# Sums of squares added on VectorE, and the opening of a decoder kernel ordered by hand

## The chip, the cores and the metric

One core of one Trainium2 chip runs the program. The metric is the device time of one launch in microseconds; several runs give a median. The profile beside it is one execution, recorded engine by engine: TensorE (PE, with its weight loads PEld), VectorE (DVE), ScalarE (ACT), GpSimd (POOL) and the queues that issue transfers (SPq for SyncE's).

## What is computed

Two macaron layers over 256 tokens of width 1024. Each layer is: half-step SwiGLU FFN, token mixer, half-step SwiGLU FFN; the first mixer is a Mamba-2 scan, the second a sliding-window attention on shared keys and values. Every sub-layer starts with an RMS norm, and that is what the change touches:

```python
def rmsnorm(x, g):
    xf = x.astype(jnp.float32)
    y = xf * lax.rsqrt(jnp.mean(xf * xf, axis=-1, keepdims=True) + EPS)
    return (y * g.astype(jnp.float32)).astype(x.dtype)

def swiglu_half_step(h, g, w1, w3, w2):
    u = rmsnorm(h, g)
    return h + FFN_HALF * ((jax.nn.silu(u @ w1) * (u @ w3)) @ w2)
```

with D_MODEL 1024 and D_FF 2816. All arrays are float32.

## The kernel before

**Layout.** The residual stream hT is kept transposed: eight k-steps of 128 features by 256 tokens. Products are made from split operands: each float32 array is split into a high part (float32r, a rounded copy) and a low part (the rest), and one product is three matmuls, high by high, high by low, low by high (`mm3`, `wmm3`, L130 and L136).

**Weights.** They come in units of 2048 columns (1 MB). A `Unit` (L142) takes a raw buffer (three of them), issues its transfer on SyncE's queue, and is split in four parts of 512 columns: ScalarE casts wh (L164), VectorE subtracts to wl (L165). There are eight buffers each of wh and wl, of 1024 columns. A unit can be held (`hold=True`): then its parts are called by hand.

**A norm.** After a sub-layer, `Norm.step` (L259) is called for four pairs b of k-steps: VectorE adds the pair into hT, `split` (L242) makes vh on ScalarE and vl on VectorE from hT times the gain, and `square` (L249) squares the pair on ScalarE into sq, and adds it to the running sum on GpSimd (L255), folding the pair's second half onto the first at the end (L257, called the half addition below). `stats` makes the mean over features with matmuls (`pc`, `token_mean`), adds eps on VectorE (`me`) and raises to the power -1/2 on GpSimd (`rms_rstd`, L208). `scale` spreads the result over the partitions with matmuls (`pb`, `spread`) and copies it to SBUF (rsb). Chunks 0 and 1 of an FFN start on vh and vl, before the scale is known, and are scaled at the gate; later chunks use the normalized uTh and uTl.

**An FFN.** `run_ffn` (L294) runs over eleven chunks of 256 inner features and two halves f of each. `up(c, f)` makes w1 and w3 products in one PSUM tile pm (48 matmuls); `gate` applies silu and the product and splits the result (ghl); `flush` makes the down products into four acc banks. For chunk 0, f = 0 goes k-step by k-step over both weights w, the others weight by weight. `later(n, fn)` puts stats and scale n matmuls further on in TensorE's order: 60 and 84 in most FFNs, 114 and 134 in the first.

**The opening.** x is loaded in two halves into xin, one of the three raw buffers. TensorE transposes it (`turn_x`, four pairs, px), vh and vl are made straight from px, chained with the splits of chunk 0's two held units; pairs 2 and 3 are turned at k-steps 3 and 5 of the first `up`, and at k-step 7 `keep_x` copies px to hT on VectorE and squares hT.

**What sets the order.** A scheduler orders each engine's instructions by program order as priority and by when their data is expected; `issue_after` (and `behind`, `after_mm`) adds an order on one engine by hand. Each engine then works its list strictly in order.

Of the kernel before, what the change touches and what calls it, by code (L numbers as in the profile page):

```python
# [40 lines left out]
def yoco_kernel(ctx: ExitStack, tc: tile.TileContext, a: dict, out: bass.AP):  # L41
# [16 lines left out]
    xin = rawp.tile([P, NT, D], F32, tag="raw", name="xin")  # L58
# [138 lines left out]

    def gain_cols(g):
        n = g.shape[0]
        pg = ps_mm.tile([P, n], F32, tag="mm", name=nm("pg"))  # L200
        nc.tensor.transpose(pg, g, ident[:n, :n])
        gc = const.tile([P, n], F32, name=nm("gcol"))
        nc.scalar.copy(gc, pg)
        gcols.append(gc)

    def rms_rstd(ms_ap, w, name):
        r = sb.tile([P, w], F32, tag=f"rstd{w}", name=nm(name), bufs=2)
        nc.gpsimd.tensor_tensor(out=r, in0=ms_ap, in1=mhalf[:, :w], op=ALU.pow)  # L208
        return r
# [21 lines left out]
    class Norm:  # L231
        def __init__(self, gi, k0):
            self.gi, self.k0 = gi, k0
# [33 lines left out]
        def stats(self):  # L267
            pc = token_mean(self.sq, 0)
            self.me = sb.tile([P, NT], F32, tag="me", name=nm("me"), bufs=2)
            nc.vector.tensor_scalar_add(self.me, pc, EPS)  # L270
            self.rs = rms_rstd(self.me, NT, "rs")

        def keep_eps(self):
            self.eps = const.tile([P, NT], F32, name=nm("eps"))
            nc.vector.tensor_scalar_mul(self.eps, self.me, EPS)
            self.rsk = const.tile([P, NT], F32, name=nm("rsk"))
            nc.vector.tensor_copy(self.rsk, self.rs)
# [16 lines left out]
    def run_ffn(layer, j, cur, nxt, hook=None, ups=None, at=(60, 84), pre=None):  # L294
# [34 lines left out]

        def up(c, f):  # L330
            u = units(c)
            xh, xl = (cur.vh, cur.vl) if c < 2 else (uTh, uTl)
            pool, tag = (ps_acc, "acc") if c == 0 and f == 0 else (ps_mm, "mm")
            pm = pool.tile([P, 512], F32, tag=tag, name=nm("pm"))

            def one(k, w, first, stop):
                wh, wl = u[k // 4].get((k % 4) * 512 + w * 256 + f * P, P)
                wmm3(pm[:, w * 256:(w + 1) * 256], wh, wl, xh[:, k, :], xl[:, k, :], first, stop)

            if c == 0 and f == 0:  # L340
                for k in range(KT):
                    if pre and k in pre:
                        pre[k]()
                    for w in range(2):
                        one(k, w, k == 0 and w == 0, k == KT - 1 and w == 1)
            else:
                for w in range(2):
                    for k in range(KT):
                        one(k, w, k == 0, k == KT - 1)
# [35 lines left out]
        def start_gates(pm):  # L385
            if hook is not None:
                cur.keep_eps()
            pend.append((0, 0, gate(0, g00)))
            pend.append((0, 1, gate(0, pm)))
            cur.normalize()  # L390

        slow = at[1] > 96
        for c in range(NCHUNK):
            for f in range(2):
                if c == 0 and f == 0:
                    later(*stats)
                    later(*scale)
                    with tc.issue_after(pe[-1]) if pe else nullcontext():
                        g00 = up(c, f)
                    continue  # L400
                pm = up(c, f)
                if c == 0 and not slow:
                    start_gates(pm)
                if c == 0:
                    g01 = pm
                    continue
                if slow and c == 1 and f == 0:
                    start_gates(g01)
# [35 lines left out]
    def mamba(mp, cur, nxt):  # L444
# [299 lines left out]
        def y_stats(g):  # L744
            pc = token_mean(st[g][1], 1)
            me = sb.tile([P, NT], F32, tag="me", name=nm("me"), bufs=2)
            nc.vector.tensor_scalar_add(me, pc, EPS)
            st[g] = (st[g][0], rms_rstd(me, NT, "grs"))
# [83 lines left out]
    def shared_kv(ap, cur, kT, vtok, bias):  # L832
# [11 lines left out]
        for t in range(NT):  # L844
# [19 lines left out]
            nc.vector.tensor_scalar_add(ss, ss, cur.eps[:, t:t + 1])  # L864
            rk = rms_rstd(ss, 2, "rk")
# [37 lines left out]
    def attention(ap, cur, kT, vtok, bias, nxt):  # L903
# [13 lines left out]
        def q_norm(pq, t, n):  # L917
# [5 lines left out]
            nc.vector.tensor_scalar_add(ss, ss, cur.eps[:, t:t + 1])  # L923
            rq = rms_rstd(ss, 8, "rq")
# [132 lines left out]
        def stats():  # L1057
            cur.stats()
            cur.keep_eps()

# [9 lines left out]
        later(42, stats)  # L1070
# [30 lines left out]
    norms = [Norm(0, 0), Norm(1, 0), Norm(0, KT), Norm(0, 2 * KT), Norm(1, KT), Norm(0, 3 * KT)]  # L1101
# [3 lines left out]
    w13 = a["ffn_w1"][0, 0], a["ffn_w3"][0, 0]  # L1105
    ups = {0: [up_unit(*w13, 0, 0, 2, True,
                       lambda: nc.sync.dma_start(xin[:, :, 512:1024], xsrc[:, :, 512:1024]))]}
    ups[0].append(up_unit(*w13, 0, 1, 2, True))
    pxs, prev = [], []

    def turn_x(b):
        pool, tag = (ps_tr, "tr") if b < 2 else (ps_acc, "acc")
# [22 lines left out]
    run_ffn(0, 0, norms[0], norms[1], ups=ups, at=(114, 134),  # L1135
            pre={3: lambda: turn_x(2), 5: lambda: turn_x(3), 7: keep_x})
# [47 lines left out]
```

## Time and profile before

| | us |
|---|---|
| median of 3 runs | 1072.65 (1067.66 to 1075.82) |
| the profiled execution | 1073.78 |
| its span in the profile | 1072.1 |
| TensorE busy | 1048.7 |
| VectorE busy | 703.3 |
| ScalarE busy | 583.1 |
| GpSimd busy | 87.1 |

The busy share of TensorE says how long matmuls were under way, not how fast they ran: the granted clock stands in a column of its own. An idle stretch of an engine other than the one that sets the end costs nothing by itself. Waits are put down to the work that came last before the waiting instruction.

### The profile page before, as it was taken

The numbers are of one execution on the slowest core, as the hardware profiler recorded it, in microseconds if no ns is written. First come the engines' busy times: TensorE is split into PE (matmuls) and PEld (weight loads), VectorE is DVE, ScalarE is ACT, GpSimd is POOL, SyncE is SP. The second block draws the span as 40 slices with busy tenths as digits, with TensorE's granted clock in tenths as the row PEclk, the third lists the DMA queues.
The fourth block names the chain that finished last, engine by engine and source line by source line (L and its number), as shares of the span: only waits on it lengthen the run. The fifth ranks groups of instructions, "written<-read, shape, count | busy, mean of one in ns | idle before, by whom it ended". The sixth has DMA issues, their size and how long they took to land.

```text
span 1072.1 us, 20450 instructions
## 1 busy us (share of the span) xinstructions
PE 1048.7 (98%) x8262; PEld 1008.7 (94%) x8262; DVE 703.3 (66%) x1399; ACT 583.1 (54%) x1200; POOL 87.1 (8%) x103
## 2 busy tenths in 40 slices
PE   7999999999999999999999999999999999999998
PEld 6999999999899999999999999999996699999997
DVE  6955546797899897646455975654577668454543
ACT  6544545667867655545355654454467556353541
POOL 5000000103210022000000200010022030000000
PEclk9899999999999999999999999999999999999999
DMA  8566555556356374556574556485641344564641
GB/s 259 180 223 212 158 198 181 174 158 217 119 178 234 121 188 145 185 195 196 162 227 153 168 197 197 159 279 169 222 158 40 118 144 149 181 217 136 211 143 40
DMA packets 138861, 187.32 MB, mean 175 GB/s; under 512 B 4876, under 2 KB 120752, under 8 KB 138768
## 3 DMA queue, kind: packets, MB, share of 16 engines
q1 hardware_dynamic: 136432, 179.32, 51.2%
q0 software_dynamic: 2288, 6.69, 2.2%
q8 instruction: 64, 1.05, 0.4%
q14 instruction: 29, 0.24, 0.1%
q10 hardware_dynamic: 48, 0.02, 0.0%
HBM read 184.90 MB, written 1.11 MB: 174 GB/s over the span
## 4 chain that ended last, share of the span: by engine, by line
PE 89%; DVE 5%; POOL 2%; ACT 2%; DMA 1%; issue 1%; SPq 0%; DVEq 0%; ACTq 0%
PE pm L103 44%; PE acc L103 23%; PE pp L103 8%; PE pa L103 5%; PE pq L101 2%; DVE wl L165 2%; POOL sq L255 1%; PE pa L101 1%; PE pz L103 1%; PE py L103 1%; PE ps L101 1%; PE po L101 1%; DVE sp L954 1%; PE pkv L103 1%; DVE zs L735 1%
## 5 line engine op out<-in xcount | busy, mean ns | idle before, releaser
L165 DVE TENSOR_TENSOR wl<-raw,wh 128x512 fp32r<-128x512 f32 x676 | 440.2, 699 | 147.5 <-ACT wh L164 146.8
L164 ACT CAST wh<-raw 128x512 fp32r<-128x512 f32 x676 | 380.2, 619 | 203.8 <-PE pm L103 104.3
L103 PE MATMUL pm<-uTh,wh 128*128 128x256 f32 x1152 | 323.3, 281 | 0.0
L103 PE MATMUL pm<-uTl,wh 128*128 128x256 f32 x1152 | 323.2, 281 | 0.0
L103 PE MATMUL pm<-uTh,wl 128*128 128x256 f32 x1152 | 323.1, 281 | 0.0
L103 PEld LDWEIGHTS pm<-uTh,wh 128*128 128x128 f32 x1152 | 217.2, 189 | 0.9 <-issue 0.2
L103 PEld LDWEIGHTS pm<-uTl,wh 128*128 128x128 f32 x1152 | 216.8, 188 | 0.6
L103 PEld LDWEIGHTS pm<-uTh,wl 128*128 128x128 f32 x1152 | 217.1, 188 | 0.0
L103 PE MATMUL acc<-ghl,wh 128*128 128x256 f32 x1056 | 190.6, 282 | 0.0
L103 PEld LDWEIGHTS acc<-ghl,wh 128*128 128x128 f32 x1056 | 162.2, 188 | 0.0
L103 PE MATMUL acc<-ghl,wl 128*128 128x256 f32 x528 | 148.7, 282 | 0.0
L323 DVE TENSOR_TENSOR g<-pm,sl 128x256 f32<-128x256 f32 x72 | 30.4, 422 | 135.8 <-ACT sl L321 135.8
L321 ACT ACTIVATE sl<-pm 128x256 f32<-128x256 f32 x72 | 27.4, 380 | 164.2 <-PE pm L103 164.2
L103 PEld LDWEIGHTS acc<-ghl,wl 128*128 128x128 f32 x528 | 99.4, 188 | 0.0
L103 PE MATMUL pp<-uTh,wh 128*128 128x256 f32 x288 | 81.8, 286 | 1.9 <-ACT uTh L291 1.4
L103 PE MATMUL pp<-uTl,wh 128*128 128x256 f32 x288 | 81.6, 284 | 0.4 <-DVE uTl L292 0.2
L103 PE MATMUL pp<-uTh,wl 128*128 128x256 f32 x288 | 81.1, 282 | 0.0
L103 PE MATMUL pm<-vh,wl 128*128 128x256 f32 x256 | 75.8, 297 | 2.1 <-DVE wl L165 2.1
L103 PE MATMUL pm<-vh,wh 128*128 128x256 f32 x256 | 76.3, 298 | 0.2 <-ACT wh L164 0.2
L103 PE MATMUL pm<-vl,wh 128*128 128x256 f32 x256 | 75.5, 295 | 0.8 <-DVE vl L244 0.8
L255 POOL TENSOR_TENSOR sq<-sq,sq 128x512 f32<-128x512 f32 x18 | 30.7, 1707 | 520.4 <-ACT sq L251 520.4
L103 PE MATMUL acc<-wh,ghl 128*128 128x512 f32 x176 | 58.1, 394 | 0.0
(236 smaller groups left out, 1480.1 us busy)
## 6 DMA issues: line engine op xcount, KB each, us to landing
raw<-in_ffn_w_dram SPq DMA_DIRECT2D x172, 512.0 KB, 4.9
raw<-in_ffn_w_dram SPq DMA_DIRECT2D x44, 1024.0 KB, 5.2
raw<-in_ssm_w_in_dram SPq DMA_DIRECT2D x16, 1024.0 KB, 5.5
raw<-in_ssm_w_out_dram SPq DMA_DIRECT2D x8, 1024.0 KB, 5.0
raw<-in_ssm_w_in_dram SPq DMA_DIRECT2D x8, 512.0 KB, 4.7
pr<-pdram POOLq DMA_DIRECT2D x8, 512.0 KB, 4.3
raw<-in_w_q_dram SPq DMA_DIRECT2D x4, 1024.0 KB, 4.9
raw<-in_w_o_dram SPq DMA_DIRECT2D x4, 1024.0 KB, 4.9
```

The source lines that it names most:

```text
L101: r = op(*args, **kw)
L103: r = op(*args, **kw)
L164: return (nc.scalar.copy(wh, rs).ins, nc.vector.tensor_sub(wl, rs, wh.bitcast(F32)).ins)
L165: nc.vector.tensor_sub(wl, rs, wh.bitcast(F32)).ins)
L255: nc.gpsimd.tensor_add(self.sq, self.sq, sq)
L321: nc.scalar.activation(sl, pm[:, 0:256], AF.Silu)
L323: nc.vector.tensor_mul(g, pm[:, 256:512], sl)
L735: nc.vector.tensor_mul(zs[:, j, :], y1, zs[:, j, :])
L954: chain[1] = op(*args, **kw).ins
```

## The change

- `Norm.square` adds the squares on VectorE instead of GpSimd.
- `rms_rstd` takes over the addition of eps; a norm that needs eps and its scale later (`want_eps`) keeps them right in `stats`.
- xin moves to a pool of its own, `xp`, which also holds a zeroed tile `dummy` and four tiles for x's squares, and is closed behind the first FFN. Mamba's pool is opened behind it.
- `keep_warm(10)` issues ten 128x128 float32 matmuls of `dummy` by itself ahead of everything else on TensorE.
- In every FFN chunk 0 is made by `up_first`: k-step by k-step, both halves f and both weights per step. In the first FFN chunk 1's f = 0 goes k-step by k-step too.
- In the first FFN chunk 1's two units are held as well. `keep_x` chains, on ScalarE and VectorE each: the splits of its first unit, x's squares straight from px (ScalarE), their additions (VectorE), the splits of the second unit, and the copies of px to hT, now on ScalarE. x's pairs 2 and 3 are turned at k-steps 1 and 3, stats and scale come at 128 and 142.

```diff
-    xin = rawp.tile([P, NT, D], F32, tag="raw", name="xin")
+    xpool = ExitStack()
+    xp = xpool.enter_context(tc.tile_pool(name="xp", bufs=1))
+    xin = xp.tile([P, NT, D], F32, name="xin")
+    dummy = xp.tile([P, P], F32, name="dummy")
+    nc.vector.memset(dummy, 0.0)
...
+    def keep_warm(n):
+        pw = ps_mm.tile([P, P], F32, tag="mm", name=nm("pw"))
+        for i in range(n):
+            nc.tensor.matmul(pw, dummy, dummy, start=True, stop=True)
...
-    def rms_rstd(ms_ap, w, name):
+    def rms_rstd(src, w, name, eps=EPS):
+        me = sb.tile([P, w], F32, tag=f"me{w}", name=nm("me"), bufs=2)
+        nc.vector.tensor_scalar_add(me, src, eps)
         r = sb.tile([P, w], F32, tag=f"rstd{w}", name=nm(name), bufs=2)
-        nc.gpsimd.tensor_tensor(out=r, in0=ms_ap, in1=mhalf[:, :w], op=ALU.pow)
+        nc.gpsimd.tensor_tensor(out=r, in0=me, in1=mhalf[:, :w], op=ALU.pow)
...
-            nc.gpsimd.tensor_add(self.sq, self.sq, sq)
+            nc.vector.tensor_add(self.sq, self.sq, sq)
             if b == 3:
-                nc.gpsimd.tensor_add(self.sq[:, 0:S], self.sq[:, 0:S], self.sq[:, S:2 * S])
+                nc.vector.tensor_add(self.sq[:, 0:S], self.sq[:, 0:S], self.sq[:, S:2 * S])
...
+            self.rs = rms_rstd(pc, NT, "rs")
+            if self.want_eps:
+                self.eps = const.tile([P, NT], F32, name=nm("eps"))
+                nc.vector.tensor_scalar(out=self.eps, in0=pc, scalar1=EPS, scalar2=EPS,
+                                        op0=ALU.add, op1=ALU.mult)
+                self.rsk = const.tile([P, NT], F32, name=nm("rsk"))
+                nc.vector.tensor_copy(self.rsk, self.rs)
...
+        def up_one(c, f, pm, k, w, first, stop):
+            xh, xl = (cur.vh, cur.vl) if c < 2 else (uTh, uTl)
+            wh, wl = units(c)[k // 4].get((k % 4) * 512 + w * 256 + f * P, P)
+            wmm3(pm[:, w * 256:(w + 1) * 256], wh, wl, xh[:, k, :], xl[:, k, :], first, stop)
+
+        def up_first():
+            pms = [ps_acc.tile([P, 512], F32, tag="acc", name=nm("pm")),
+                   (ps_acc if pre else ps_mm).tile([P, 512], F32, tag="acc" if pre else "mm", name=nm("pm"))]
+            for k in range(KT):
+                if pre and k in pre:
+                    pre[k]()
+                for f in range(2):
+                    for w in range(2):
+                        up_one(0, f, pms[f], k, w, k == 0 and w == 0, k == KT - 1 and w == 1)
+            return pms
...
         def up(c, f):
...
+            pm = ps_mm.tile([P, 512], F32, tag="mm", name=nm("pm"))
+            if c == 1 and f == 0 and pre:
                 for k in range(KT):
...
                     for w in range(2):
...
+                        up_one(c, f, pm, k, w, k == 0 and w == 0, k == KT - 1 and w == 1)
+                return pm
...
+    keep_warm(10)
...
+    ups[1] = [up_unit(*w13, 1, h, 2, True) for h in range(2)]
     pxs, prev = [], []
 
+    def chained(unit, c):
+        with behind(*prev[-1]):
+            prev.append(unit.part(c))
...
     def keep_x():
+        for c in range(0, 2048, 512):
+            chained(ups[1][0], c)
+        sqs = [xp.tile([P, 2 * S], F32, name=f"xsq{b}") for b in range(4)]
         for b, px in enumerate(pxs):
-            with behind(*prev[-1]):
-                nc.vector.tensor_copy(hT[:, 2 * b:2 * b + 2, :], px)
-                n0.square(b)
+            with behind(prev[-1][0]):
+                v = nc.scalar.activation(sqs[b], px.rearrange("p i s -> p (i s)"), AF.Square).ins
+            prev.append((v, prev[-1][1]))
+        for b in range(1, 4):
+            with behind(prev[-1][1]):
+                w = nc.vector.tensor_add(sqs[0], sqs[0], sqs[b]).ins
+            prev.append((prev[-1][0], w))
+        with behind(prev[-1][1]):
+            w = nc.vector.tensor_add(sqs[0][:, 0:S], sqs[0][:, 0:S], sqs[0][:, S:2 * S]).ins
+        prev.append((prev[-1][0], w))
+        n0.sq = sqs[0]
+        for c in range(0, 2048, 512):
+            chained(ups[1][1], c)
+        for b in (3, 0, 1, 2):
+            with behind(prev[-1][0]):
+                v = nc.scalar.copy(hT[:, 2 * b:2 * b + 2, :], pxs[b]).ins
+            prev.append((v, prev[-1][1]))
 
     turn_x(0)
     turn_x(1)
-    run_ffn(0, 0, norms[0], norms[1], ups=ups, at=(114, 134),
-            pre={3: lambda: turn_x(2), 5: lambda: turn_x(3), 7: keep_x})
+    run_ffn(0, 0, norms[0], norms[1], ups=ups, at=(128, 142),
+            pre={1: lambda: turn_x(2), 3: lambda: turn_x(3), 7: keep_x})
+    xpool.close()
```

## Rows read from the trace of the kernel before

**Rows 1.** Page, parts 1 and 2: busy time by engine; granted clock in tenths.

```profile
PE 1048.7 (98%) x8262; PEld 1008.7 (94%) x8262; DVE 703.3 (66%) x1399; ACT 583.1 (54%) x1200; POOL 87.1 (8%) x103
...
PEclk9899999999999999999999999999999999999999
```

**Rows 2.** Waits of TensorE, whole span: us in total, times, longest us.

```profile
PE px L1116 <- DMA xin<-in_x_dram: 5.1, 1, 5.1
PE pc L103 <- POOL sq L257: 3.6, 3, 1.7
...
PE pm L103 <- DVE wl L165: 2.1, 2, 1.1
...
PE pm L103 <- DVE vl L244: 0.8, 2, 0.4
```

**Rows 3.** Stretches: length, busy us (x) by engine, granted clock, DMA share, GB/s.

```profile
20.00:40.00 20.00, 17.65 (x114) 16.70 (x114) 17.04 (x27) 12.71 (x25) 6.56 (x5) 0.83 0.63 216
...
60.00:80.00 20.00, 20.00 (x171) 20.00 (x170) 9.83 (x18) 9.50 (x19) 0.00 (x0) 1.00 0.57 184
...
400.00:420.00 20.00, 18.29 (x141) 18.08 (x140) 12.69 (x23) 11.61 (x22) 8.27 (x5) 0.91 0.44 160
```

**Rows 4.** Timeline of ScalarE, second FFN: start, us, instruction.

```profile
405.39 0.62 ACT L251 ACTIVATE sq<-hT 128x512 f32<-128x512 f32 x1
```

**Rows 5.** Timeline of GpSimd, the same stretch; idle before and its releaser in brackets.

```profile
406.08 4.58 POOL L255 TENSOR_TENSOR sq<-sq,sq 128x512 f32<-128x512 f32 x1 [2.71 <-ACT sq L251]
410.75 0.72 POOL L257 TENSOR_TENSOR sq<-sq 128x256 f32<-128x256 f32 x1
412.48 0.71 POOL L208 TENSOR_TENSOR rs<-me,mhalf 128x2 f32<-128x2 f32 x1 [1.01 <-DVE me L270]
```

**Rows 6.** Additions of squares by line: ns min/median/max, first and last start us, form.

```profile
L255 POOL TENSOR_TENSOR sq<-sq,sq x18: 1279/1302/4583, 20.1 to 877.1; 128x512 f32<-128x512 f32 x18
...
L740 DVE TENSOR_TENSOR sq<-sq,sq x4: 679/685/693, 281.3 to 381.4; 128x512 f32<-128x512 f32 x4
L741 DVE TENSOR_TENSOR sq<-sq x4: 413/416/424, 282.0 to 382.6; 128x256 f32<-128x256 f32 x4
```

**Rows 7.** Timeline of VectorE, second FFN's beginning.

```profile
406.44 3.09 DVE L165 TENSOR_TENSOR wl<-raw,wh 128x512 fp32r<-128x512 f32 x5
```

**Rows 8.** Timeline of TensorE, the same stretch: pc, the next matmul, pb.

```profile
411.52 0.61 PE L103 MATMUL pc<-mean,sq 128*128 128x1 f32 x4 [1.71 <-POOL sq L257]
411.99 0.37 PE L103 MATMUL pm<-vh,wh 128*128 128x256 f32 x1
...
416.45 0.61 PE L103 MATMUL pb<-ident,rs 128*128 128x128 f32 x4
```

**Rows 9.** Timeline of TensorE in the opening.

```profile
5.09 1.09 PE L1116 MATMUL px<-ident,xin 128*128 128x128 f32 x4 [5.09 <-DMA xin<-in_x_dram]
...
7.72 0.58 PE L103 MATMUL pm<-vh,wh 128*128 128x256 f32 x1 [0.25 <-ACT wh L164]
...
24.26 0.39 PE L103 MATMUL pm<-vh,wl 128*128 128x256 f32 x1 [1.07 <-DVE wl L165]
...
31.91 1.05 PE L103 MATMUL pb<-ident,rs 128*128 128x128 f32 x4
...
40.67 0.41 PE L103 MATMUL acc<-ghl,wh 128*128 128x256 f32 x2
```

**Rows 10.** Waits of SyncE's queue, 0 to 62 us: total us, times, longest us.

```profile
SPq L151 <- PE px L1116: 4.2, 1, 4.2
```

**Rows 11.** Timeline of ScalarE in the opening.

```profile
18.30 0.62 ACT L164 CAST wh<-raw 128x512 fp32r<-128x512 f32 x1 [2.37 <-DMA raw<-in_ffn_w_dram]
```

**Rows 12.** Timeline of VectorE in the opening.

```profile
15.97 0.69 DVE L165 TENSOR_TENSOR wl<-raw,wh 128x512 fp32r<-128x512 f32 x1
16.58 2.48 DVE L1130 COPY hT<-px 128x512 f32<-128x512 f32 x4
...
20.52 7.72 DVE L165 TENSOR_TENSOR wl<-raw,wh 128x512 fp32r<-128x512 f32 x7 [0.87 <-ACT wh L164]
```

More of the change, by code (lines that the diff above doesn't have):

```diff
@@ L231, in yoco_kernel, with __init__ @@
     class Norm:
-        def __init__(self, gi, k0):
-            self.gi, self.k0 = gi, k0
+        def __init__(self, gi, k0, want_eps=False):
+            self.gi, self.k0, self.want_eps = gi, k0, want_eps
         def g(self, d):
@@ L268, in stats @@
             pc = token_mean(self.sq, 0)
[L269 to L277, printed above, removed]
+            self.rs = rms_rstd(pc, NT, "rs")
[5 more added lines that the diff above has]
+                nc.vector.tensor_copy(self.rsk, self.rs)
         def scale(self):
@@ L328, in gate @@
             return gh, gl
-        def up(c, f):
[L331 to L340, printed above, removed]
+        def up_one(c, f, pm, k, w, first, stop):
[12 more added lines that the diff above has]
+            return pms
+        def up(c, f):
+            pm = ps_mm.tile([P, 512], F32, tag="mm", name=nm("pm"))
+            if c == 1 and f == 0 and pre:
                 for k in range(KT):
-                    if pre and k in pre:
-                        pre[k]()
                     for w in range(2):
[L345 to L349, printed above, removed]
+                        up_one(c, f, pm, k, w, k == 0 and w == 0, k == KT - 1 and w == 1)
+                return pm
+            for w in range(2):
+                for k in range(KT):
+                    up_one(c, f, pm, k, w, k == 0, k == KT - 1)
             return pm
@@ L383, in run_ffn, with start_gates @@
         pend = []
[L385 to L389, printed above, removed]
+        def start_gates():
+            for f in range(2):
+                pend.append((0, f, gate(0, g0[f])))
             cur.normalize()
@@ L398, in run_ffn @@
                     with tc.issue_after(pe[-1]) if pe else nullcontext():
-                        g00 = up(c, f)
+                        g0 = up_first()
+                    if not slow:
+                        start_gates()
+                if c == 0:
                     continue
                 pm = up(c, f)
[L402 to L406, printed above, removed]
                 if slow and c == 1 and f == 0:
-                    start_gates(g01)
+                    start_gates()
                 g = gate(c, pm)
@@ L745, in y_stats @@
             pc = token_mean(st[g][1], 1)
[L746 to L748 removed]
+            st[g] = (st[g][0], rms_rstd(pc, NT, "grs"))
         def y_scale(g):
@@ L863, in shared_kv @@
                                     axis=AX.X, op=ALU.add)
-            nc.vector.tensor_scalar_add(ss, ss, cur.eps[:, t:t + 1])
-            rk = rms_rstd(ss, 2, "rk")
+            rk = rms_rstd(ss, 2, "rk", cur.eps[:, t:t + 1])
             kf = kd[:, 256:384].rearrange("p (g d) -> p g d", g=2)
@@ L922, in q_norm @@
                                     axis=AX.X, op=ALU.add)
-            nc.vector.tensor_scalar_add(ss, ss, cur.eps[:, t:t + 1])
-            rq = rms_rstd(ss, 8, "rq")
+            rq = rms_rstd(ss, 8, "rq", cur.eps[:, t:t + 1])
             nc.vector.tensor_mul(qn.rearrange("p (g d) -> p g d", g=8),
@@ L1069, in attention @@
             nc.scalar.activation(warm, mhalf[:, 0:1], AF.Exp)
-        later(42, stats)
+        later(42, cur.stats)
         strict[0] = True
@@ L1099, in attention @@
             nxt.step(b, accs[b], 1.0)
-    norms = [Norm(0, 0), Norm(1, 0), Norm(0, KT), Norm(0, 2 * KT), Norm(1, KT), Norm(0, 3 * KT)]
+    norms = [Norm(0, 0), Norm(1, 0), Norm(0, KT), Norm(0, 2 * KT, True), Norm(1, KT, True), Norm(0, 3 * KT)]
     n0 = norms[0]
@@ L1108, in yoco_kernel @@
     ups[0].append(up_unit(*w13, 0, 1, 2, True))
+    ups[1] = [up_unit(*w13, 1, h, 2, True) for h in range(2)]
     pxs, prev = [], []
+    def chained(unit, c):
+        with behind(*prev[-1]):
+            prev.append(unit.part(c))
     def turn_x(b):
-        pool, tag = (ps_tr, "tr") if b < 2 else (ps_acc, "acc")
+        pool, tag = ((ps_tr, "tr"), (ps_acc, "acc"), (ps_acc, "acc"), (ps_mm, "mm"))[b]
         px = pool.tile([P, 2, S], F32, tag=tag, name=nm("px"))
```

3 lines of the change are left out of this document (removed).

## The prediction, made before the changed kernel ran

> **What bounds the kernel now.** I read the busy shares first. TensorE is busy for 98% of the span, VectorE for 66% and ScalarE for 54% [rows 1]: nothing can be gained but where TensorE idles or where its clock is low. The list of TensorE's waits gives the idle time: 5.1 us until x has landed, 3.6 us in three waits of pc (the per-token mean of squares) for the GpSimd additions, 2.1 us for weight low halves (wl), 0.8 us for activation low halves (vl) [rows 2]. The table by stretches shows the rest. An undisturbed stretch of 20 us holds 171 matmuls, 0.117 us each; 20 to 40 us holds 114 at a granted clock of 0.83, and 400 to 420 us holds 141 at 0.91 [rows 3]. So the opening and the beginnings of some FFNs lose time twice: in a stall, and in the half-clock stretch (1.2 instead of 2.4 GHz) that follows it.
>
> The second FFN shows how. The last squares leave ScalarE at 405.39 + 0.62 = 406.01 us [rows 4]. The GpSimd addition behind them starts at 406.08 and takes 4.58 us, where the median of its kind is 1.30 [rows 5, 6]; meanwhile VectorE runs five subtractions in 3.09 us, from 406.44 to 409.53 [rows 7]. The half addition follows, to 411.47, and pc starts at 411.52 after a stall of 1.71 us [rows 5, 8]. From 411.99 to 416.45 there stand 24 matmuls [rows 8], which at 0.117 are 2.8 us and took 4.5: 1.6 us lost to the clock. One such place costs 1.7 + 1.6 = 3.3 us. The waits list has three: the longest is 1.7, and two of that size and one of 0.2 make its 3.6 [rows 2]; the second large one is the last FFN's, the small one the opening's.
>
> **Part 1: the additions on VectorE.** The change removes three GpSimd additions and a half addition per norm and adds three of 0.685 us and one of 0.416 on VectorE, whose rows are mamba's own sums of squares [rows 6]: 2.5 us per norm at most. The first two of each norm fall into idle time (VectorE is busy 12.69 of the 20 us [rows 3]); the last two go behind the vl split, so squares done at 406.01 are summed by about 406.5 + 0.69 + 0.42 = 407.6, if the scheduler puts them ahead of the five subtractions. Pc is due at 411.52 − 1.71 = 409.8: no stall, 2.2 us to spare. If they stand behind the subtractions, they end at 409.53 + 1.1 = 410.6, and 0.8 us of stall stay. I take the first, since the five belong to code that comes later in the program. What loses cover is those five, 1.1 us later; the matmuls that read them come after half of chunk 0, whose new order asks for a k-step's data every 1.4 us, 12 × 0.117, instead of 0.7. That also removes the 0.8 us of vl waits, which stand in the third FFN's chunk 0. Gain: 2 × 3.3 + 0.8 = 7.4 us, between 1.8 (two stalls shortened by 0.9 each, clock and vl waits as before) and 7.4.
>
> The Trainium skill (SBUF — State Buffer, Who interferes with whom) says that of a VectorE operation with two SBUF inputs and a GpSimd one, whichever starts first holds the shared port pair for its whole instruction and the other is blocked. By that rule the addition, once started, would have run its 1.30 us and the half addition would have ended near 408.5, with no stall to remove; the 4.58 us against five VectorE instructions at 0.62 each [rows 5, 7] show GpSimd losing turn after turn, so I go by the row.
>
> The merged eps code keeps its count: me moves into the helper; one scalar multiply becomes one two-operation instruction. Nothing.
>
> **Part 2: the opening.** Today x's transposes start at 5.09, the first real matmul at 7.72, and the first down matmul (acc) at 40.67 [rows 9]. Between 7.72 and 40.67 stand 192 up matmuls, 22.5 us at 0.117; eight transposes, about 1.1 us, half of what the first eight take at the lower clock (1.09 us for four [rows 9]); pc, and pb (the spread of the scale), about 1 us. That is 24.6 of 33 us: 8.4 us are lost. The cause is chunk 1. Its first weight unit waits for x's buffer: the DMA queue waits 4.2 us for the transposes, ScalarE 2.37 us for the data, until 18.30 [rows 10, 11]. VectorE copies x to hT for 2.48 us meanwhile, and starts chunk 1's seven further subtractions at 20.52, mixed with ScalarE squares that wait for GpSimd [rows 12]. TensorE stalls 1.07 us at 24.26, and once more, then runs at half clock: the two pb matmuls still take 1.05 us at 31.91 [rows 9].
>
> With x in a pool of its own, three raw buffers serve weights, and chunk 1's first unit is issued without that 4.2 us wait; its second waits only for unit 0's splits. On the chained order: the last subtraction of chunk 0 starts at 15.97 [rows 12] and ends near 16.6; four subtractions of chunk 1 at 0.62 take it to 19.1; three additions and a half to about 21.6, since ScalarE's four squares come out between 18 and 20.3; the second unit's four subtractions to 24.1. The four hT copies cost ScalarE 4 × 0.62 = 2.5 us behind its last cast, to about 24.5, before chunk 1's second half needs that bank.
>
> TensorE then: 7.72, plus about 0.5 us for the first low halves, plus 96 × 0.117 = 11.2 and 1.1 for transposes: chunk 0 ends at 20.5. Chunk 1's first half, k by k, takes 5.6 us and pc 0.5: to 26.6. Its k-step 4 is due at 20.5 + 4 × 0.7 = 23.3, and its data is there at 22.2; k-step 7 is due at 25.4, data at 24.1. Pc comes 32 matmuls in, at 24.2; its inputs are there at 21.6. VectorE's me and GpSimd's pow (0.71) [rows 5] need 1.1 us after pc, and pb comes 16 matmuls, 1.9 us, behind. Pb 0.4, the second half 5.6, mamba's ptc transposes and small change 0.8: down matmuls start near 33.4 instead of 40.7. Gain 7.3; lower bound 2 (warm start only, stall and half clock stay), upper 8.4.
>
> Dummies: ten fp32 128x128 matmuls. Two of that form take 0.61 us at full clock and 1.05 at half [rows 8, 9], so ten take 3.1 to 5.3 us. They need one memset only; if they start near 1 us, they end between 4.1 and 6.3, against x at 5.09: 0 to 1.2 us late. I take 0, as overlapped starts make the upper end unlikely. What they warm is part of the 20.5 above.
>
> **Sum.** The profiled run took 1073.78 us, 1.7 around a span of 1072.1, and 1.1 above the median of 1072.65. Gains 7.4 + 7.3 = 14.7; I give back 0.5 for the new order's slightly slower matmul pace at bank changes. 1073.78 − 14.2 = **1059.6, say 1060 us**.
>
> **Rivals.**
> *The opening keeps a stall* (chance 0.2). The chain is strict: one late weight unit holds squares, copies and gates behind it; or mamba's small preloads on GpSimd, which reuse x's memory, now sit in front of the pow, or land late under a transpose. Against: the data is 1.1 and 1.3 us early at k-steps 4 and 7 above. With 2 instead of 7.3 from it: 1065.
> *The additions come late* (0.1): behind the subtractions, 1.8 instead of 7.4: 1065.2. For: the scheduler filled exactly that gap with subtractions.
> *The additions remove nothing* (0.05), because the stall's real cause is not the GpSimd addition's length, as the skill's port rule would have it: only opening and vl waits, 7.3 + 0.8 − 0.5: 1066. Against: the 4.58 us row.
> *Slower* (0.05): VectorE becomes the bound where a norm's step meets weight splits. Price per norm 2.1 us of additions on the path and 1.6 of half clock behind the stall, 3.7; five such norms make 18.5, against which 14.2 stand: 1078. It decides once four of the five are hit. Against: from 400 to 420 us, the stretch with such a step, VectorE is busy 12.7 of 20 us [rows 3].
> *Forecast* (0.6): both parts work, 1055 to 1063.
>
> **Numbers.** The range 1055 to 1068 holds the forecast, the first three rivals and leaves the slower case and some of the tails: 0.85. A measurement of this kernel tells about 1%, 10.7 us, from no change, that is below 1061.9. Most of the forecast case lies there (0.54 of its 0.6), its rest, and the three middle rivals (0.35), lie within 1%; slower by over 1% is the last rival's upper part. Faster 0.54, same 0.42, slower 0.04.
>
> **What would show it.** Pc's waits for sums of squares gone or under 0.3 us, and granted clock 1.00 where it was 0.91 near 400 and 880 us; the stretch 20 to 40 with some 165 matmuls; the first acc matmul near 33 us; no GpSimd additions over squares; chunk 1's first cast before 16.5 us instead of 18.3. I am wrong if pc still waits, now for VectorE, if TensorE waits for wl or vl in mamba's or attention's beginnings, or if the first acc matmul stays past 37 us.

## The result, and the profile after

The changed kernel took 1061.65 us (median of 8 runs, 1060.33 to 1064.87) against 1070.31 of the kernel before (8 runs, 1066.92 to 1075.82): a ratio of 0.9919, with a 95% interval from 0.9894 to 0.9944. The prediction was 1060 in a range of 1055 to 1068, so the time lies in it. The gain of 0.8% is short of the 1% that the prediction set as the bound of "faster", the case to which it gave 0.54; the result falls into "within 1%", which had 0.42. The profiled execution took 1061.67 us with a span of 1060.0. The profiled spans are 12.1 us apart, the medians 8.7, because the profiled execution of before (1073.78) was a long one: 3.5 us above that median.

The page of the changed kernel, parts 1 and 2, answers to [rows 1]: GpSimd is down from 87.1 to 53.0 us, TensorE busy for 99%, and no slice shows a granted clock below 0.9.

```profile
PE 1044.2 (99%) x8282; PEld 1006.2 (95%) x8282; DVE 701.4 (66%) x1420; ACT 582.7 (55%) x1204; POOL 53.0 (5%) x79
...
PEclk9999999999999999999999999999999999999999
```

TensorE's waits (us in total, times, longest) answer to [rows 2]. The three waits of pc for GpSimd are gone, and so are those of pm for weight and activation low halves. Three others were there before too, though [rows 2] doesn't show them: pa for weight low halves, pc for mamba's own sum (L752) and pp. New are 1.1 us ahead of the dummies and 1.0 of pb for the pow.

```profile
PE pa L107 <- DVE wl L169: 1.8, 1, 1.8
PE px L1125 <- DMA xin<-in_x_dram: 1.5, 1, 1.5
PE pc L107 <- DVE sq L752: 1.4, 1, 1.4
PE pp L107 <- ACT uTh L300: 1.4, 1, 1.4
PE pw L205 <- DVE dummy L62: 1.1, 1, 1.1
PE pb L107 <- POOL rs L219: 1.0, 1, 1.0
```

The stretches, to be held against [rows 3], whose columns they have: 160 matmuls instead of 114 from 20 to 40 us, 170 instead of 141 from 400 to 420, both at full clock. The stretches of mamba shown, from 260 to 280 and from 300 to 320, are short of the 171 of an undisturbed one.

```profile
20.00:40.00 20.00, 19.04 (x160) 18.84 (x160) 17.90 (x36) 16.40 (x34) 5.81 (x12) 1.00 0.59 186
260.00:280.00 20.00, 18.06 (x149) 16.91 (x148) 16.25 (x31) 17.10 (x36) 5.57 (x7) 0.96 0.50 156
...
300.00:320.00 20.00, 18.18 (x148) 17.43 (x147) 17.71 (x27) 16.05 (x34) 4.08 (x5) 0.91 0.62 184
400.00:420.00 20.00, 20.00 (x170) 20.00 (x170) 18.75 (x38) 12.94 (x25) 1.12 (x1) 1.00 0.62 211
```

**Where the 12.1 us arose.** I take the start of the same matmul in both timelines, before less after. At the first down matmul (acc) the changed kernel leads by 6.4 us (40.67 [rows 9] to 34.27), at mamba's first pb by 5.8. At pc of mamba's second group (326.34, before 330.74) only 4.4 are left; the stretch from 300 to 320 above ran at 0.91. The second FFN's beginning brings the lead from 4.5 to 7.8 (pb at 408.65, before at 416.45 [rows 8]), the chunks behind it to 9.1, the last FFN's beginning from 9.3 to 12.8 (pb at 874.64, before at 887.43), and the end has 12.1. Three of these matmuls in the changed kernel:

```profile
34.27 0.40 PE L107 MATMUL acc<-ghl,wh 128*128 128x256 f32 x2
...
405.33 0.50 PE L107 MATMUL pc<-mean,sq 128*128 128x1 f32 x4
...
408.65 0.49 PE L107 MATMUL pb<-ident,rs 128*128 128x128 f32 x3
```

The second FFN's beginning on VectorE (start, us, instruction) shows the additions of the new kind: 0.68 and 0.42 us, the last ending at 402.77, between weight subtractions and ahead of five more. Pc starts at 405.33 without a wait, 2.56 us later.

```profile
401.15 0.68 DVE L266 TENSOR_TENSOR sq<-sq,sq 128x512 f32<-128x512 f32 x1
401.75 0.68 DVE L169 TENSOR_TENSOR wl<-raw,wh 128x512 fp32r<-128x512 f32 x1
402.35 0.42 DVE L268 TENSOR_TENSOR sq<-sq 128x256 f32<-128x256 f32 x1
402.69 3.09 DVE L169 TENSOR_TENSOR wl<-raw,wh 128x512 fp32r<-128x512 f32 x5
```

### The profile page after: what moved, and what is told of

The parts are those of the page before. It is cut to its first block, busy times and chain, and to the rows that moved or that the text cites. A ratio compares the mean times of both kernels' runs of the same rounds, so it can differ in the third digit from the quotient of the medians.

```text
span 1060.0 us, 20512 instructions
## 1 busy us (share of the span) xinstructions
PE 1044.2 (99%) x8282; PEld 1006.2 (95%) x8282; DVE 701.4 (66%) x1420; ACT 582.7 (55%) x1204; POOL 53.0 (5%) x79
## 4 chain that ended last, share of the span: by engine, by line
PE 93%; DVE 4%; ACT 1%; DMA 1%; issue 1%; POOL 0%; SPq 0%; ACTq 0%; DVEq 0%; POOLq 0%
PE pm L107 47%; PE acc L107 23%; PE pp L107 8%; PE pa L107 5%; PE pq L105 2%; PE pa L105 1%; DVE wl L169 1%; PE pz L107 1%; PE py L107 1%; PE ps L105 1%; PE po L105 1%; DVE sp L961 1%; DMA xin<-in_x_dram 1%; PE pkv L107 1%; DVE zs L746 1%
## 5 line engine op out<-in xcount | busy, mean ns | idle before, releaser
L169 DVE TENSOR_TENSOR wl<-raw,wh 128x512 fp32r<-128x512 f32 x676 | 431.6, 685 | 140.9 <-ACT wh L168 140.1
L107 PE MATMUL pm<-vh,wh 128*128 128x256 f32 x256 | 73.2, 286 | 0.0
L107 PE MATMUL pm<-vl,wh 128*128 128x256 f32 x256 | 72.4, 283 | 0.0
L107 PE MATMUL pm<-vh,wl 128*128 128x256 f32 x256 | 72.3, 283 | 0.0
L107 PEld LDWEIGHTS pp<-uTh,wh 128*128 128x128 f32 x288 | 54.4, 190 | 2.6 <-ACT uTh L300 1.5
```

The lines of the kernel that those rows point to most:

```text
L107: r = op(*args, **kw)
L169: nc.vector.tensor_sub(wl, rs, wh.bitcast(F32)).ins)
```

## Is it the additions, and is it more than noise?

My theory was the prediction's: two independent gains, 7.4 us from the additions and 7.3 from the opening. Its first rival was that the difference lies in half-clock stretches that fall otherwise from one execution to the next. One run is the unchanged kernel again; the next has the additions alone:

```
-            nc.gpsimd.tensor_add(self.sq, self.sq, sq)
+            nc.vector.tensor_add(self.sq, self.sq, sq)
-                nc.gpsimd.tensor_add(self.sq[:, 0:S], self.sq[:, 0:S], self.sq[:, S:2 * S])
+                nc.vector.tensor_add(self.sq[:, 0:S], self.sq[:, 0:S], self.sq[:, S:2 * S])
```

> The kernel before once more, unchanged: what is asked is how its own runs differ. Theory A (half-clock stretches come and go): its runs spread over some 8 us as before (1067 to 1076), and the longer ones have the lower mean granted clock, about 0.992 against 0.996; then a stall of 1.7 us costs between 1.7 us (no half clock behind it) and 3.3 us, and what the change brought by medians lies between 2 x 1.7 and 2 x 3.3 for the additions. Theory B (something else, such as transfers): the spans differ at the same clock.

Measured: 1073.24 us (12 runs), ratio 0.9998 (0.9982 to 1.0013). Its profile, span 1070.4, has the stretch of 400 to 420 at another clock than [rows 3]:

```profile
20.00:40.00 20.00, 17.36 (x123) 16.27 (x122) 18.17 (x30) 13.71 (x27) 6.52 (x5) 0.91 0.63 216
400.00:420.00 20.00, 18.31 (x154) 18.09 (x153) 13.62 (x25) 12.91 (x25) 8.05 (x5) 1.00 0.45 155
880.00:900.00 20.00, 19.23 (x137) 18.71 (x138) 14.43 (x30) 10.66 (x20) 1.42 (x2) 0.91 0.52 173
```

The stall from 400 to 420 us is there in the same size, but the half-clock stretch that I had put behind each stall is there in one execution and not in the next; behind the last FFN's stall (880 to 900) both have it. Among 29 runs of the kernel before on this chip the mean granted clock and the time go together, from 0.995 and 1067.6 us to 0.989 and 1078.5. So one profile is no measure of a few us; what follows goes by medians, and by waits that come back from profile to profile.

> Of the change only this: the running sum of squares is added on VectorE in every norm; opening and chunk order are those of before. Theory A (the GpSimd addition is held up beside VectorE's subtractions and pc waits for it): the two waits of pc of 1.7 us near 411 and 882 us are gone, and 3.4 to 6.6 us with them, ratio 0.994 to 0.997; the 0.2 us wait in the opening changes little. Rival (the additions move and the stall stays, because the wait's real cause is another): pc still waits, 1.000. Second rival (VectorE's added 2.5 us per norm delay low halves): new waits of TensorE for wl or vl, ratio over 1.000.

Measured: 1063.96 us (1063.25 to 1064.57, 6 runs), ratio 0.9913 (0.9889 to 0.9936): a gain above the one expected. On another chip, as adds_only_2, with the changed kernel beside it:

> The additions alone once more, for the comparison on one chip: 0.991 of the kernel before, as measured, if that does not depend on the chip. The profile asks whether mamba's wait of pc for its own sum of squares is again 0.5 us (1.4 in the kernels before and after) and whether the stretch 280 to 300 us is again at full clock; if both differ between two looks at one program, they are chance and not the change.

Measured: 1063.96 again (1062.85 to 1065.04), ratio 0.9936 (0.9913 to 0.9958).

> The changed kernel once more, beside the one with the additions alone on the same chip. Theory O (the opening's lead is real and lasts): down matmuls start 6 us earlier than with the additions alone, and the end is 5 to 6 us earlier, ratio to it about 0.995. Theory M (part of the lead is given back in mamba, where VectorE and ScalarE set the pace and a half-clock stretch falls differently): the end is 2 to 3 us earlier, ratio to it 0.997 to 0.998. Rival: nothing is left of it, 1.000.

Measured: 1062.18 (1060.3 to 1065.49), ratio 0.9919 (0.9892 to 0.9946). So the additions alone bring 9.9 and 6.5 us, where I had 7.4 for them with the new chunk order; everything else adds 1.8 us (by medians; the runs of the two kernels overlap), where I had 7.3. TensorE's waits with the additions alone:

```profile
PE px L1116 <- DMA xin<-in_x_dram: 5.1, 1, 5.1
PE pa L103 <- DVE wl L165: 1.8, 1, 1.8
PE pp L103 <- ACT uTh L291: 1.4, 1, 1.4
PE pm L103 <- DVE wl L165: 1.4, 2, 0.8
...
PE pc L103 <- DVE sq L741: 0.5, 1, 0.5
```

No pc waits for GpSimd any more, and pm's waits for vl are gone without the new chunk order (in the next kernel, with the new order and the additions on GpSimd, they are gone too: either edit removes them). Before, TensorE's wait at 600.83 ended with a vl instruction that had taken 1.50 us, where its like take 0.47, beside a GpSimd addition. And mamba's own sum is late by 0.5 us instead of 1.4, though nothing there was changed; this comes back below.

## Is the GpSimd addition slow because of VectorE?

> The changed kernel with the five norms' additions back on GpSimd (the opening keeps its own on VectorE). Theory A: pc waits again, 1.7 us twice, with or without the half clock: 3.4 to 6.6 us slower than the changed kernel, 1065 to 1068 us, and the ratio to before is that of the opening and the chunk order alone, about 0.994. Rival (new chunk order already gives the additions the time they lacked): within 1 us of the changed kernel, since chunk 0's new order asks for fewer subtractions at that point.

This is the changed kernel with the same two lines back on GpSimd. Measured: 1073.95 us (12 runs), ratio 1.0006 (0.9987 to 1.0025): everything else in the change is worth nothing as long as the additions stay on GpSimd, where I had expected 1065 to 1068. Its first down matmul comes at 34.38, a lead of 6.3 us, as in the changed kernel; then it is lost, 2.4 of it at the second FFN's beginning (4.2 ahead at 382.31, 1.8 at pb, 414.64). Waits of TensorE, and the second FFN's beginning on GpSimd and VectorE:

```profile
PE pc L107 <- POOL sq L268: 5.8, 2, 2.9
PE pb L107 <- POOL rs L219: 2.1, 2, 1.1
```

```profile
401.86 5.78 POOL L266 TENSOR_TENSOR sq<-sq,sq 128x512 f32<-128x512 f32 x1 [2.70 <-ACT sq L262]
...
402.23 4.29 DVE L169 TENSOR_TENSOR wl<-raw,wh 128x512 fp32r<-128x512 f32 x7
```

Before, the addition took 4.58 us beside five subtractions in 3.09 [rows 5, 7]; here 5.78 beside seven in 4.29. Two more subtractions, 1.20 us, and the addition is 1.20 us longer: here it waits until the run of VectorE instructions is over. My reading, which no run tests apart, is that what frees the weight buffers sooner (here the new opening or the chunk order) puts more subtractions into that place, so the same addition costs more.

It is not so everywhere. Of the 18 additions of [rows 6] in the kernel before, only two took 4.58 us, the second FFN's and the last FFN's; the other sixteen took 1.28 to 1.55, and where a subtraction began beside one of them, it was the subtraction that waited, for instance in the opening, where it takes 1.63 us instead of 0.68:

```profile
22.11 1.55 POOL L255 TENSOR_TENSOR sq<-sq,sq 128x512 f32<-128x512 f32 x1 [0.74 <-ACT sq L251]
22.58 1.63 DVE L165 TENSOR_TENSOR wl<-raw,wh 128x512 fp32r<-128x512 f32 x1
```

So the prediction's "turn after turn" holds for two places of 18. In both, VectorE's splits were under way when the addition began; but that is so for some of the sixteen as well (here a subtraction runs from 21.84 to 22.52), so what decides is not shown. The Trainium skill (SBUF — State Buffer, Who interferes with whom) says that a VectorE instruction with two SBUF inputs contends with a GpSimd one that reads SBUF. These rows agree. The rule from that section that the prediction set against the row, that whoever starts first holds the pair for its whole instruction, is written there for VectorE's two-port modes; it fits the sixteen, but gives no length like 4.58 or 5.78 us: by it the addition's turn would have come at the end of the one VectorE instruction under way, not of seven.

The other way to take the stall away is to ask for the sum later. Here the additions stay on GpSimd, in the kernel before:

```
-    def run_ffn(layer, j, cur, nxt, hook=None, ups=None, at=(60, 84), pre=None):
+    def run_ffn(layer, j, cur, nxt, hook=None, ups=None, at=(74, 95), pre=None):
```

> The kernel before with stats and scale later in TensorE's order: 74 and 95 matmuls on instead of 60 and 84, in the four FFN beginnings that have the default; the additions stay on GpSimd. 14 matmuls are 1.64 us at 0.117. Theory A (the sum is 1.7 us late and nothing else is wrong): pc's two long waits shrink to 0.1 us and no half clock follows; same gain as the additions alone, ratio 0.994 to 0.997. Rival (the addition is held up as long as subtractions follow, so it gets later too): pc waits on, ratio 0.998 to 1.000.

Measured: 1066.99 us (12 runs), ratio 0.9944 (0.9925 to 0.9963). Pc's waits for GpSimd are gone and 400 to 420 us holds 169 matmuls at full clock. Asking 14 matmuls later gives some two thirds of what moving the additions gave on that chip (0.0056 of 0.0087), so the wait, not GpSimd's work as such, is most of what the additions cost. The waits for vl (0.8 us) and mamba's pc (1.4) are still in its list.

## What in the opening is worth something?

In the kernel before, the two stalls of 1.07 us that the prediction saw (TensorE's 24.26 in [rows 9] and one at 26.55) end with subtractions that the additions of x's squares on GpSimd had held up: the one at 22.58 above, and one of 1.63 at 24.87. That is why seven subtractions took 7.72 us [rows 12]. With the additions alone moved, the two stalls are still 0.80 and 0.59, now behind VectorE's own additions, and the first down matmul comes at 40.35 and 40.14 in two profiles, before at 40.67 and 39.53.

In the changed kernel VectorE's first subtractions of chunk 1 stand behind chunk 0's last (four of the five at 15.70), with the additions of x's squares behind them:

```profile
15.70 3.10 DVE L169 TENSOR_TENSOR wl<-raw,wh 128x512 fp32r<-128x512 f32 x5
18.77 2.29 DVE L1146 TENSOR_TENSOR xsq<-xsq,xsq 128x512 f32<-128x512 f32 x3
21.09 0.42 DVE L1149 TENSOR_TENSOR xsq<-xsq 128x256 f32<-128x256 f32 x1
21.43 2.49 DVE L169 TENSOR_TENSOR wl<-raw,wh 128x512 fp32r<-128x512 f32 x4
```

The next kernel is the one with the additions alone, and x in a pool of its own:

```
-    xin = rawp.tile([P, NT, D], F32, tag="raw", name="xin")
+    xpool = ExitStack()
+    xp = xpool.enter_context(tc.tile_pool(name="xp", bufs=1))
+    xin = xp.tile([P, NT, D], F32, name="xin")
...
+    xpool.close()
```

> The kernel with the additions alone moved to VectorE, and x in a pool of its own; the rest of the opening as before. My theory of the opening is that chunk 1's first weight unit came late because it waited for x's buffer: then its first cast starts before 16.5 us instead of 18.3, the stall of 1.1 us near 24.3 goes, and the first down matmul comes at 37 to 38.5 us instead of 40.1 to 40.4; the whole 1062 or a little below, against 1064.0 for the additions alone. Rival: the buffer only hides the real limit, which is the work that ScalarE and VectorE have on x itself (copies to hT, squares, additions) ahead of chunk 1's splits: then the first cast comes earlier, but the first down matmul stays at 39.5 us or later and the whole at 1063.5 to 1064.5.

Measured: 1064.28 us (4 runs), ratio 0.9922 (0.9895 to 0.9950), the same as the additions alone. On ScalarE and VectorE:

```profile
15.88 0.62 ACT L166 CAST wh<-raw 128x512 fp32r<-128x512 f32 x1 [1.39 <-DMA raw<-in_ffn_w_dram]
16.41 0.47 ACT L245 ACTIVATE vh<-px,gcol 128x256 fp32r<-128x256 f32 x1
16.77 2.17 ACT L166 CAST wh<-raw 128x512 fp32r<-128x512 f32 x4
...
18.13 2.48 DVE L1132 COPY hT<-px 128x512 f32<-128x512 f32 x4
...
21.50 1.28 DVE L167 TENSOR_TENSOR wl<-raw,wh 128x512 fp32r<-128x512 f32 x2
```

Chunk 1's first cast comes at 15.88, 2.4 us earlier than [rows 11], and the stall near 24.3 falls to 0.16 us, as expected. But of chunk 1's subtractions only the first comes earlier; the second, which stood at 20.52 before [rows 12], starts at 21.50, because VectorE copies x to hT and adds squares in between, and TensorE waits 1.44 us for wl at 26.98. A new stall comes on top: that first cast waits 1.39 us for its transfer, and chunk 0's last split (vh, and the cast at 16.77) stands behind it in ScalarE's list, so TensorE waits 1.03 us at 17.43. The first down matmul comes at 41.04, no earlier than 40.35 with the additions alone; without the new stall it would be near 40, still not the 37 to 38.5 expected. My theory that x's buffer alone made chunk 1 late falls: the buffer was late, but behind it VectorE's own order was the limit. What the order gives without its warm start:

```
-    keep_warm(10)
```

> The changed kernel without the ten matmuls on zeros. Theory W (they bring TensorE's clock up before the first real matmul): x's first eight transposes take 2.2 us instead of 1.3, first matmuls are 0.21 us apart instead of 0.12, and the first down matmul comes about 1 to 1.5 us later; 1 us slower at the end, ratio to the changed kernel 1.001, no more than can be told. Rival (they only stand in the way of x's transposes): the first transpose starts at 5.1 instead of 5.4 us and the first down matmul no later.

Measured: 1064.74 us (1061.95 to 1065.14, 6 runs), ratio 0.9937 (0.9913 to 0.9960). The first down matmul comes at 36.73, where the five profiles with the dummies and the same opening have 34.27 to 36.40 (the latest of them, sel_late below, ran at a clock of 0.81 from 10 to 15 us), and the two of the kernel before 39.53 and 40.67. So at that point the order is worth 2.8 to 3.9 us and the dummies 0.3 to 2.5. By medians the dummies are worth 2.6 us on that chip, with intervals that overlap; without them the kernel is no faster at the end than the additions alone there (1064.74 and 1063.96).

Pb's new wait of 1.0 us has this on GpSimd, in the changed kernel:

```profile
25.73 0.56 POOL L462 DMA_DIRECT2D rows<-in_ssm_conv_w_dram  x1 [0.16 <-POOL rows L465]
26.28 0.51 POOL L463 DMA_DIRECT2D rows<-in_ssm_conv_b_dram  x1
26.81 0.75 POOL L219 TENSOR_TENSOR rs<-me,mhalf 128x2 f32<-128x2 f32 x1
```

Me was there at 25.64; two of mamba's preloads stand in front of the pow. They had waited for pc, which reads x's squares from the pool whose memory mamba's pool takes over. Issued behind it:

```
+        held = ExitStack()
+        held.enter_context(behind(pows[0]))
     (the preloads of mamba's rows, biases and wdt)
+        held.close()
```

> The changed kernel with mamba's small preloads on GpSimd put behind the first norm's pow in GpSimd's list. In the changed kernel two memsets and two transfers stand in front of that pow, from 25.23 to 26.81 us, and pb waits 1.0 us for it. Theory P (they are the cause): pow starts near 25.7, pb waits 0.1 us or not at all, down matmuls start near 33.3 instead of 34.3, 0.5 to 1 us at the end. Rival: me is late as well (it stands behind subtractions on VectorE), and pb waits 0.5 us or more still.

Measured: 1061.09 us (1060.03 to 1062.42), ratio 0.9910 (0.9887 to 0.9932), beside 0.9919. Pb comes 0.38 us earlier and its wait is down from 1.0 to 0.2 us, but nothing of it can be told at the end. Last, the old order of chunk 0 in the three later FFNs:

```
-                for f in range(2):
+                for f in range(2 if pre else 1):
...
+            if not pre:
+                for w in range(2):
+                    for k in range(KT):
+                        up_one(0, 1, pms[1], k, w, k == 0, k == KT - 1)
```

> The changed kernel, with the first chunk of the three later FFNs in its old order (one half after the other; the first FFN keeps the new one). If the new order is worth the 0.8 us that I put on it, the waits for low halves of activations (vl) come back with 0.8 us and weight low halves (wl) with up to 2 us in pm, and the whole is 1 to 3 us above the changed kernel's, 1063 to 1065. Rival: with the additions on VectorE those waits cost nothing that the order saves, or the order costs as much at bank changes: no difference, 1061 to 1062.5.

Measured: 1060.54 us (4 runs), ratio 0.9897 (0.9863 to 0.9931): no difference that can be told from the changed kernel (on this chip only the ratio to before compares the two), and no waits of pm for vl or wl came back. The new order in the later FFNs removes nothing that the additions had not removed.

## Where the rest of the opening's lead went

The changed kernel is 6.1 us ahead of the one with the additions alone at the first down matmul, 5.2 at mamba's first pb (212.34 and 217.58), 2.8 at its second (282.78 and 285.59), and 2.4 at the end. Between the two pb stands the sum whose wait differs. VectorE's multiplications of y by zs (ns min/median/max, first and last start), in the changed kernel:

```profile
L746 DVE TENSOR_TENSOR zs<-y,zs x4: 409/849/2237, 268.9 to 274.4; 128x256 f32<-128x256 f32 x4
```

and with the additions alone:

```profile
L735 DVE TENSOR_TENSOR zs<-y,zs x4: 411/629/1280, 274.0 to 278.2; 128x256 f32<-128x256 f32 x4
```

The one of 2237 runs from 271.26, and GpSimd beside it makes selections on the decays:

```profile
271.56 1.08 POOL L714 TENSOR_SCALAR_AFFINE_SELECT em<-pr 128x1024 f32<-128x1024 f32 x1
272.58 0.64 POOL L716 TENSOR_SCALAR_AFFINE_SELECT em<-pr 128x512 f32<-128x512 f32 x1
```

Here it is VectorE that waits, until both selections are done, though its multiplication began 0.3 us before the first of them (as it did with the additions alone, where it took 0.41). The kernel before has the same 2.2 us and the same wait of 1.4 us. Of the twelve profiles up to here nine have them; the three without are the two of the additions alone and the one with x's own pool. From mamba's first pb to its second the nine take 70.1 to 71.9 us, the three 68.0 to 69.2. That makes the additions alone look better, and the opening worse, than they are. To test it, the changed kernel with mamba's second group of selections held behind the pow of the first group's norm:

```
         stage_b(0)
-        exps(1)
...
+        def y_stats_exps():
+            y_stats(0)
+            with behind(pows[-1]):
+                exps(1)
```

> The changed kernel, with mamba's GpSimd selections for its second group of decays held behind the pow of the first group's norm. In the changed kernel, as in the one before, a VectorE multiplication of y by zs that takes 0.41 us elsewhere takes 2.24 there, while GpSimd runs two selections; in the two runs with the additions alone none is over 1.3, the first group's pc waits 0.5 us instead of 1.4, and the stretch from 280 to 300 us is at full clock instead of 0.91 to 0.96. My theory is that this collision is where the opening's lead was lost (6.3 us at the first down matmul, 2.5 at the end): then no multiplication is over 1.4 us, pc's wait is 0.6 or less, 280 to 300 is at a clock of 1.00, and the whole is 2 to 2.6 us below the changed kernel: 1058 to 1060. Rival: the lead goes because VectorE and ScalarE set the pace of mamba whatever is taken away (VectorE is busy 18 to 19 of 20 us at 220 to 240): the wait moves to another place, and the whole stays at 1061 to 1062.5.

Measured: 1056.55 us (1055.98 to 1060.79, 4 runs), ratio 0.9860 (0.9828 to 0.9893): 5 to 6 us below the changed kernel as measured on other chips (4.0 below the run with the old chunk order on this one), about twice what I expected. Mamba's first pb to its second takes 67.6 us. The profile is of the longest of the four executions, 1060.79 us, whose first down matmul came at 36.40. The multiplications and the stretches:

```profile
L748 DVE TENSOR_TENSOR zs<-y,zs x4: 415/416/416, 272.0 to 274.8; 128x256 f32<-128x256 f32 x4
```

```profile
260.00:280.00 20.00, 20.00 (x177) 19.38 (x176) 18.53 (x39) 16.61 (x34) 0.96 (x1) 1.00 0.38 109
280.00:300.00 20.00, 19.90 (x169) 19.70 (x168) 19.65 (x41) 19.54 (x43) 10.19 (x10) 1.00 0.52 183
300.00:320.00 20.00, 20.00 (x178) 19.43 (x177) 17.22 (x28) 15.07 (x33) 4.13 (x5) 1.00 0.65 193
```

Pc's wait is gone, and with it the wait of pa for weight low halves (1.8 us), which I had left out. In the changed kernel it ends at 312.29, and of the multiplications ahead of it, beside the next selections, one took 1.86 us:

```profile
309.44 1.86 DVE L746 TENSOR_TENSOR zs<-y,zs 128x256 f32<-128x256 f32 x1
...
311.56 1.28 DVE L169 TENSOR_TENSOR wl<-raw,wh 128x512 fp32r<-128x512 f32 x2
```

With the selections held, the weight subtractions there are done by 304.8, ahead of the next selections, so that these hold up no subtraction that TensorE waits for. The 300 to 320 stretch has 178 matmuls instead of 148. Part is given back: ScalarE copies cbs late, and ptx waits 1.9 us for it at 328.34.

> The changed kernel, with the selections of mamba's second group held as in the run before this one, and mamba's own preloads on GpSimd issued behind the first norm's pow. If both stalls are real losses, the sum of the two: pb near 27.2 instead of 27.6, first down matmul at or before 34, and 0.3 to 0.7 us less than the run before this: 1057.5 to 1059.5. Rival: nothing more than the selections alone, since TensorE's half-clock stretches fall as they will and take up half a microsecond.

Both edits together: 1056.64 us (1056.14 to 1058.29, 4 runs), ratio 0.9856 (0.9824 to 0.9889). The pow's place adds nothing that can be told, as before. These two are the fastest of the study, 1.4% below the kernel before.

## The prediction, step by step

*Bound by TensorE's idle time and clock.* Right, as far as the runs show: the gains are removed waits, with or without a half-clock stretch behind them, and in the opening the pace of the first matmuls.

*Additions, 7.4 us.* Right in mechanism, near in size. The sum is ready 2.56 us ahead of pc, where I had 2.2 to spare; the two places gained 3.3 and 3.5 us in the profiles against 3.3 each, and the vl waits 1.3 against 0.8. Two things were wrong beside that. The half clock behind a stall (1.6 of each 3.3) is not the stall's fixed price: the kernel before, profiled again, had none from 400 to 420. And the vl waits are the GpSimd additions' doing too: they go by the additions alone as well as by chunk 0's order: from pb of the second FFN to pc of the third, the additions alone, the changed kernel and the one with the old order each gain 1.3 us. The order has no term of its own.

*Opening, 7.3 us.* Near in size at the first down matmul, wrong in cause and in what reaches the end. The first down matmul came at 34.27 against 33.4, pc at 24.61 against 24.2, chunk 1's first cast at about 15.6 (before 16.5, as said); of the 0.9 us missing, the pow behind two preloads is 0.38 (pow_first), the mechanism of the first rival in small. But x's own pool by itself gave nothing, and the two stalls that I put down to chunk 1's late start ended with subtractions that GpSimd's additions held up. The order by hand, squares and copies placed around the subtractions, carries more of the lead at the first down matmul than the dummies do; at the end, by medians on one chip, the changed kernel is 1.8 us ahead of the additions alone, and without the dummies it is not ahead.

*The sum.* It failed in taking the two parts as separate. Without the additions' move the opening is worth 0 (no_adds), with it 1.8 us by medians; I had 7.3. Of the 5.5 between, 0.9 were missing at the first down matmul already, 0.9 went from there to mamba (every profile with the new opening takes 178.0 to 178.2 us over that stretch, the others 177.2 to 177.4; no run followed it up), and 2.4 are the wait in mamba, with the half clock behind it, that the additions alone escaped and the changed kernel did not. These are from one profile of each; with the second profiles the 2.4 lies between 1.2 and 3.9. The rest is too small for the medians to place. By the profiles of before and after that wait cancels, since both have it: 5.8 us of opening and 8.1 of additions and vl waits (3.3, 1.3, 3.5) are 13.9, near the 14.2, and 1.8 of them were lost again, 1.4 in mamba at the lower clock.

*The base.* I subtracted 14.2 from a profiled 1073.78, which was 3.5 above the later median. By profiles, 12.1 of 14.2 us came; by medians, 8.7. By profiles the result would have been a gain of 1.1%, by medians it is 0.8%: that difference put it on the other side of the bound. That 1060 is so near to 1061.65 is partly luck: a base 3.5 us too high and a gain 5.5 us too large by medians work against each other. From the median of 1070.31 the same gains would have given 1056.1, still in the range.

*Dummies, 0 us late.* Near: they ended at 5.54 and x's transposes started at 5.37, against 5.09; 0.28 us late, and up to 0.46 in the other profiles.

*Rivals.* Slower, by VectorE as the bound: no; from 400 to 420 it is busy 18.75 us and pc waits for nothing. Additions late or without effect: no.

**Still open:** why the multiplication of y by zs is held for both selections in one kernel and passes in another, and why an addition on GpSimd waits for a whole run of subtractions in two places and has its turn in sixteen; and how much of the order's 2.8 to 3.9 us at the first down matmul is the copies on ScalarE and how much the placement of the squares, which wasn't tried apart.

## To carry to other kernels

An elementwise sum on GpSimd that a waiting matmul needs can cost not its own 1.3 us but the run of two-input VectorE instructions beside it, so changes elsewhere that lengthen that run make it dearer; where GpSimd has its turn, the VectorE work beside it pays, as the subtractions in the opening and the multiplications beside GpSimd's selections did. Look at both engines' durations beside each other before either is costed. Cost two edits together only after asking what each puts into the other's gap, and take as base a median, not the one profiled execution. Before a late buffer is blamed, look at what the next engine in the chain has in its queue ahead of the data.

## What the runs showed of the hardware that I had not expected

- GpSimd and VectorE hold each other up in both directions: an addition of 1.30 us took 4.58 beside five subtractions and 5.78 beside seven; in sixteen of 18 places it took no more than 1.55 and a subtraction of 0.68 that began beside it took up to 1.78 instead; a multiplication of 0.41 us took 2.24 beside two selections of 1.08 and 0.64. In the kernel with held selections one selection took 4.44 us, where its median is 1.07.
- After one and the same stall the half-clock stretch comes in one execution and not in another: 400 to 420 us at 0.91 and at 1.00 in two profiles of the same kernel, both with pc's waits of 3.6 us in all. The 29 executions of that kernel on one chip range over 10.9 us.
